# The odd side of a Fourier projection: three 128-column passes per weight tile, or one of 256 columns and one of 128

## The chip, the cores and the metric

The kernel runs on one core of a Trainium2 chip. The time is device microseconds of one execution of the program. Five engines matter here: TensorE (PE in the rows; PEld are its weight loads), VectorE (DVE), ScalarE (ACT), GpSimd (POOL) and SyncE (SP), which issues the DMAs. Each works through its own list of instructions in order and waits on semaphores where it needs another's result.

## The reference

Two layers of an encoder on 256 tokens of width 2048, in float32: a token mixer, a cross-attention on a memory, and a gated MLP. The change lies in the token mixer, in the linear map behind the Fourier branch:

```python
def fourier_mix(u):
    ug = u.astype(jnp.float32).reshape(b, s, N_FOURIER_GROUPS, FOURIER_GROUP_DIM)   # 4 groups of 256 channels
    y = jnp.fft.fft2(ug, axes=(1, 3), norm='ortho').real
    return y.reshape(b, s, F_WIDTH).astype(u.dtype)
...
    a = blocked_gqa(q, k, v) @ w_attn_o
    f = fourier_mix(uf) @ w_four_o
    g = jax.nn.sigmoid(h @ w_gate + b_gate)
    merged = g[..., :D_MODEL] * a + g[..., D_MODEL:] * f
    return merged @ w_mix_o
```

`w_four_o` has 1024 rows and 2048 columns.

## The kernel before

**Products in two halves.** Every float32 operand is split into a high part, rounded to fp32r, and a low part, the rest: `hi` and `lo`. A product is hi x hi + hi x lo + lo x hi. Weights come from HBM as tiles of 128 x 1024 (`load`, L105, four buffers `w32`), are split by ScalarE (`whi`, L121, a cast) and VectorE (`wlo`, L123, a subtraction), four buffers each, and then used as the stationary operand, 128 x 128 at a time. The activations are the moving operand and lie as [128, 2 parts, 256 tokens], so that one pass of 512 columns with the `hi` weights makes two of the three products at once, in two halves of a PSUM bank, and one pass of 256 columns with the `lo` weights makes the third (`block`, L140 and L141). `merge` (L212, L213) adds the two halves: ScalarE copies one to SBUF, VectorE adds the other.

**The Fourier branch.** The output of the two-dimensional transform has a symmetry over the tokens, so the branch keeps an even part on 129 tokens (`FE`, four groups, and `FX`, a fifth operand for the middle channels; padded to 130) and an odd part on 127 tokens (`FO`, padded to 128). Each is stored as [128, 2 parts, n]. `fourier(c)` computes 128 of the 2048 output columns. It forms sums and differences of the weights (`sd`, L754 and L755), splits them, and makes an even side with the sums (and with `FX` and a small extra weight, `wx`) and an odd side with the differences. Then f[t] = even - odd and f[256 - t] = even + odd (L782, L783), and the gate multiplies it (L786). It is a generator: at each `yield` the caller may put other work in.

In the even side a weight tile takes the two passes of `block`, 260 and 130 columns. In the odd side it takes three passes of 128 columns, (hi, part 0), (hi, part 1) and (lo, part 0), all into the same 128 columns of the same bank (L774): the bank has 512 float32 columns, of which the even side fills 260.

**Where it is called.** Two of the 16 output blocks (`EARLY`, c = 0 and 1) are computed with their gates inside attention, one `next(early)` per head, to fill TensorE there. `att_scores` makes the scores `sc` (L488) and the softmax, `att_out` transposes the probabilities (`pt`, L510), splits them (`et`, `et_lo`), multiplies by the values (`pv`, L521) and splits the result into `O`. The other 14 come after attention, in the merge loop, one turn for each c: two gate products `g` (L140, L141, 16 weight tiles each), the Fourier block, the attention projection `a` (16 weight tiles), and the merge of all into `M`.

**What sets the order.** The code is written against a framework that orders the instructions of each engine itself, by priority and by when it expects operands to be ready, and that puts in the semaphores. Tiles of a pool go round its buffers: PSUM pool `ps_mm` has four banks for `g`, `f` and `a` alike, pool `t1` five scratch buffers of 128 x 256 for gates, halves, `even`, `fo` and `ao`.

Of the kernel before, what the change touches and what calls it, by code (L numbers as in the profile page):

```python
# [16 lines left out]
P = 128  # L17
# [22 lines left out]
NE, NO = 130, 128  # L40
# [3 lines left out]
def encoder(ctx: ExitStack, tc: tile.TileContext, t, out):  # L44
    nc = tc.nc
# [42 lines left out]
    def tmp1(name, dt=F32):  # L88
        return t1.tile([P, T], dt, tag="t1", name=name)
# [4 lines left out]
    def psum(name):  # L94
        return ps_mm.tile([P, 512], F32, tag="mm", name=name)
# [4 lines left out]
    def psum_pt(name):  # L100
        return ps_pt.tile([P, 512], F32, tag="pt", name=name)

    def load(src, n=HW):
        w = wp.tile([P, HW], F32, tag="w32", name="w32", bufs=4)
        nc.sync.dma_start(w[:, :n], src)  # L105
        return w
# [465 lines left out]
    for l in range(L):  # L572
# [85 lines left out]
        for j, n, g, dst, w0 in pairs:  # L658
# [8 lines left out]
            if n is qs and j in (2, 4):  # L667

                i = j - 2
                ps = psum_pt("ps_kn")  # L670
# [13 lines left out]
        FE = [F[:, i:j].rearrange("p (s n) -> p s n", s=2) for i, j in zip(o, o[1:])]  # L684
        FX = FE.pop()
        o = [o[-1] + g * 2 * NO for g in range(5)]
        FO = [F[:, i:j].rearrange("p (s n) -> p s n", s=2) for i, j in zip(o, o[1:])]
# [61 lines left out]
        def fourier(c):  # L749


            src = load(t["w_fo"][l, c][:, :HW])
            sd = wp.tile([P, HW], F32, tag="w32", name="sd", bufs=4)
            nc.vector.tensor_add(sd[:, :512], src[:, :512], src[:, 512:])  # L754
            nc.vector.tensor_sub(sd[:, 512:], src[:, :512], src[:, 512:])  # L755
            w = Unit(None, cuts=[(0, HW)], loaded=[sd])
            w.split()
            wx = wp.tile([P, P], F32, tag="wx", name="wx")
            nc.sync.dma_start(wx, t["w_fo"][l, c][:, HW:])
            xh, xl = wx_hl[c % 2], wx_hl[2 + c % 2]  # L760
            nc.scalar.copy(xh, wx)
            nc.vector.tensor_sub(xl, wx, xh.bitcast(F32))
            ps = psum("f")
            for k in range(5):
                hi, lo = w(k * P) if k < 4 else (xh, xl)
                a = FE[k] if k < 4 else FX
                nc.tensor.matmul(ps[:, : 2 * NE], hi, a.rearrange("p s n -> p (s n)"), start=k == 0, stop=False, skip_group_check=True)
                nc.tensor.matmul(ps[:, :NE], lo, a[:, 0], start=False, stop=k == 4, skip_group_check=True)
            yield
            odd = ps[:, 2 * NE : 2 * NE + NO]  # L770
            for k in range(4):
                hi, lo = w(512 + k * P)
                for i, (x, part) in enumerate(((hi, 0), (hi, 1), (lo, 0))):
                    nc.tensor.matmul(  # L774
                        odd, x, FO[k][:, part], start=k + i == 0, stop=k == 3 and i == 2, skip_group_check=True
                    )
            yield
            even = tmp1("even")
            nc.scalar.copy(even[:, :129], ps[:, NE : NE + 129])
            nc.vector.tensor_add(even[:, :129], even[:, :129], ps[:, :129])  # L780
            f = tmp1("fo")
            nc.vector.tensor_sub(f[:, 1:128], even[:, 1:128], odd[:, :127])  # L782
            nc.vector.tensor_add(f[:, 255:128:-1], even[:, 1:128], odd[:, :127])  # L783
            nc.vector.tensor_copy(f[:, 0:129:128], even[:, 0:129:128])
            g = gates[c][1]
            nc.vector.scalar_tensor_tensor(out=g, in0=g, scalar=1.0, in1=f, op0=ALU.add, op1=ALU.mult)  # L786

        gates = [[] for _ in range(KT)]
        early = chain(*[chain(gated(c, 0), gated(c, 1), fourier(c)) for c in range(EARLY)])
        before = None  # L790
        for h in range(NH + 1):
            if h < NH:
                k = [k_hl[:, h // GRP, part] for part in range(2)]
# [20 lines left out]
        for c in range(KT):  # L814
            if c >= EARLY:
                run(chain(gated(c, 0), gated(c, 1), fourier(c)))
            scaled_split(merged(c), 0.5, M[:, c])
# [32 lines left out]
        if l == 0:  # L850
            ps = msum.ps
# [294 lines left out]
```

## Time and profile before

| what | value |
|---|---|
| runs | 3044.52, 3046.54, 3048.32 us; median 3046.54 |
| profiled execution | 3047.76 us, span 3046.0 us |
| granted TensorE clock | 0.995 of full, mean over the span |
| TensorE busy | 98% of the span |
| VectorE busy | 69% |
| ScalarE busy | 56% |

The span runs from the first to the last instruction in the trace; the time has 1.8 us more around it. Busy is the time in which an engine has at least one instruction under way; for TensorE instructions overlap, so the sum of their durations says little, and the distance from one start to the next says what a pass costs.

### The profile page before, as it was taken

Reading aid. Unit: us, or ns where it says so; the run is one execution under the profiler, and the core shown is the slowest. Engines: PE = TensorE matmul, PEld = TensorE weight load, DVE = VectorE, ACT = ScalarE, POOL = GpSimd, SP = SyncE. Lnnn points to the kernel's source line nnn. Section 1 sums busy time; section 2 is a strip of 40 time slices with the busy share of each in tenths; the row PEclk is TensorE's granted clock in tenths of the full one; section 3 lists DMA queues with packets and bytes.
Section 4 is the critical chain, followed back from the end, with each engine's and each line's share of the span. In section 5 each row is a group of like instructions: output and inputs, shape, how many; then the busy total and the mean of one; then the engine's idle time right before and its main releaser. Section 6 shows DMA issues by size and latency. Waiting matters only on the chain.

```text
span 3046.0 us, 43076 instructions
## 1 busy us (share of the span) xinstructions
PE 2981.9 (98%) x16016; PEld 2536.8 (83%) x16016; DVE 2113.3 (69%) x3358; ACT 1712.6 (56%) x2812; POOL 39.1 (1%) x40
## 2 busy tenths in 40 slices
PE   8999999999999999999989999999999999999998
PEld 6888888877788888888868888888777888888887
DVE  5678777675785766757766687776657857677676
ACT  5676544565654545545556865454657545455454
POOL 1000000010000000000000000000000000000000
PEclk9999999999999999999999999999999999999999
DMA  7543555654456565565745435556645565655655
GB/s 256 172 155 112 191 195 191 204 191 150 162 194 193 187 184 193 181 197 186 223 153 174 160 106 192 189 193 205 201 149 167 187 196 186 185 194 184 196 186 161
DMA packets 162499, 554.44 MB, mean 182 GB/s; under 512 B 18160, under 2 KB 22512, under 8 KB 162160
## 3 DMA queue, kind: packets, MB, share of 16 engines
q1 hardware_dynamic: 162288, 551.68, 56.0%
q8 instruction: 125, 2.05, 0.3%
q14 instruction: 86, 0.70, 0.1%
HBM read 549.51 MB, written 2.10 MB: 181 GB/s over the span
## 4 chain that ended last, share of the span: by engine, by line
PE 73%; DVE 2%; ACT 2%; issue 1%; DMA 0%; POOLq 0%; DVEq 0%; SPq 0%; ACTq 0%
PE up L140 21%; PE up L141 10%; PE y L342 7%; PE y L344 6%; PE y L343 6%; PE g L140 4%; PE a L140 2%; PE g L141 2%; PE qk L140 2%; DVE wlo L123 1%; PE as L344 1%; PE as L342 1%; PE a L141 1%; PE as L343 1%; PE kx L140 1%; PE as L200 1%
## 5 line engine op out<-in xcount | busy, mean ns | idle before, releaser
L123 DVE TENSOR_TENSOR wlo<-w,whi 128x1024 fp32r<-128x1024 f32 (+1 forms) x993 | 1195.6, 1208 | 699.1 <-ACT whi L121 692.4
L121 ACT CAST whi<-w 128x1024 fp32r<-128x1024 f32 (+1 forms) x993 | 1026.7, 1036 | 1008.1 <-PE up L140 385.1
L140 PE MATMUL up<-A_ff,whi 128*128 128x512 f32 x2688 | 946.6, 398 | 0.8 <-ACT whi L121 0.8
L141 PE MATMUL up<-A_ff,wlo 128*128 128x256 f32 x2688 | 752.9, 280 | 0.5 <-DVE wlo L123 0.5
L140 PEld LDWEIGHTS up<-A_ff,whi 128*128 128x128 f32 x2688 | 505.0, 188 | 125.2 <-ACT whi L121 1.6
L141 PEld LDWEIGHTS up<-A_ff,wlo 128*128 128x128 f32 x2688 | 507.1, 189 | 1.7 <-DVE wlo L123 1.4
L140 PE MATMUL g<-A_mix,whi 128*128 128x512 f32 x1024 | 365.6, 399 | 0.0
L141 PE MATMUL g<-A_mix,wlo 128*128 128x256 f32 x1024 | 288.9, 282 | 0.0
L342 PE MATMUL y<-whi,G 128*128 128x512 f32 x704 | 274.1, 389 | 0.0
L343 PE MATMUL y<-wlo,G 128*128 128x512 f32 x704 | 274.0, 389 | 0.0
L344 PE MATMUL y<-whi,G 128*128 128x512 f32 x704 | 274.0, 389 | 0.0
L140 PEld LDWEIGHTS g<-A_mix,whi 128*128 128x128 f32 x1024 | 192.5, 188 | 45.7
L140 PE MATMUL qk<-A_mix,whi 128*128 128x512 f32 x640 | 227.6, 399 | 0.0
L141 PEld LDWEIGHTS g<-A_mix,wlo 128*128 128x128 f32 x1024 | 193.6, 189 | 0.0
L140 PE MATMUL a<-O,whi 128*128 128x512 f32 x512 | 183.7, 402 | 0.0
L141 PE MATMUL qk<-A_mix,wlo 128*128 128x256 f32 x640 | 179.8, 281 | 0.0
L344 PEld LDWEIGHTS y<-whi,G 128*128 128x128 f32 x704 | 132.2, 188 | 27.6
L342 PEld LDWEIGHTS y<-whi,G 128*128 128x128 f32 x704 | 132.2, 188 | 27.5
L343 PEld LDWEIGHTS y<-wlo,G 128*128 128x128 f32 x704 | 132.1, 188 | 27.2
L141 PE MATMUL a<-O,wlo 128*128 128x256 f32 x512 | 143.8, 281 | 0.0
L140 PEld LDWEIGHTS qk<-A_mix,whi 128*128 128x128 f32 x640 | 120.2, 188 | 27.5
L141 PEld LDWEIGHTS qk<-A_mix,wlo 128*128 128x128 f32 x640 | 121.0, 189 | 0.1
(267 smaller groups left out, 4096.3 us busy)
## 6 DMA issues: line engine op xcount, KB each, us to landing
w<-in_w_up SPq DMA_DIRECT2D x336, 512.0 KB, 3.8
w<-in_w_dn SPq DMA_DIRECT2D x160, 512.0 KB, 3.8
w<-in_w_g SPq DMA_DIRECT2D x128, 512.0 KB, 4.4
w<-in_w_qk SPq DMA_DIRECT2D x80, 512.0 KB, 4.4
w<-in_w_ao SPq DMA_DIRECT2D x64, 512.0 KB, 3.7
w<-in_w_mo SPq DMA_DIRECT2D x64, 512.0 KB, 4.3
w<-in_w_vu SPq DMA_DIRECT2D x47, 512.0 KB, 4.8
w<-in_w_fo SPq DMA_DIRECT2D x32, 512.0 KB, 3.7
```

What stands on the lines that cost most here:

```text
L121: nc.scalar.copy(hi[:, :m], w[:, :m])
L123: nc.vector.tensor_sub(lo[:, :m], w[:, :m], hi[:, :m].bitcast(F32))
L140: nc.tensor.matmul(ps, hi, a, start=first, stop=False, skip_group_check=True)
L141: nc.tensor.matmul(ps[:, :T], lo, a[:, 0:T], start=False, stop=last, skip_group_check=True)
L200: nc.tensor.matmul(pss[j], ah, lo, start=False, stop=False)
L342: nc.tensor.matmul(ps, ah, hi, start=first, stop=False)
L343: nc.tensor.matmul(ps, ah, lo, start=False, stop=False)
L344: nc.tensor.matmul(ps, al, hi, start=False, stop=last)
```

## The change

The odd side gets a bank of its own (`fodd`) and the form of the even side: per weight tile one pass of 256 columns with the `hi` weights over both parts of `FO`, into two halves of that bank, and one pass of 128 columns with the `lo` weights. Both sides run in one loop, with a `yield` after each as before. Since the odd product now lies in two halves, it is brought together as the even one was: a copy by ScalarE and an add by VectorE, into a fifth kind of scratch tile, `odd`.

```diff
-            ps = psum("f")
-            for k in range(5):
-                hi, lo = w(k * P) if k < 4 else (xh, xl)
-                a = FE[k] if k < 4 else FX
-                nc.tensor.matmul(ps[:, : 2 * NE], hi, a.rearrange("p s n -> p (s n)"), start=k == 0, stop=False, skip_group_check=True)
-                nc.tensor.matmul(ps[:, :NE], lo, a[:, 0], start=False, stop=k == 4, skip_group_check=True)
-            yield
-            odd = ps[:, 2 * NE : 2 * NE + NO]
-            for k in range(4):
-                hi, lo = w(512 + k * P)
-                for i, (x, part) in enumerate(((hi, 0), (hi, 1), (lo, 0))):
+            pse, pso = psum("f"), psum("fodd")
+            for ps, ops, c0, nt in ((pse, FE + [FX], 0, NE), (pso, FO, 512, NO)):
+                for k, a in enumerate(ops):
+                    hi, lo = w(c0 + k * P) if k < 4 else (xh, xl)
                     nc.tensor.matmul(
-                        odd, x, FO[k][:, part], start=k + i == 0, stop=k == 3 and i == 2, skip_group_check=True
+                        ps[:, : 2 * nt], hi, a.rearrange("p s n -> p (s n)"), start=k == 0, stop=False, skip_group_check=True
                     )
-            yield
-            even = tmp1("even")
-            nc.scalar.copy(even[:, :129], ps[:, NE : NE + 129])
-            nc.vector.tensor_add(even[:, :129], even[:, :129], ps[:, :129])
+                    nc.tensor.matmul(
+                        ps[:, :nt], lo, a[:, 0], start=False, stop=k == len(ops) - 1, skip_group_check=True
+                    )
+                yield
+            even, odd = tmp1("even"), tmp1("odd")
+            for x, ps, nt in ((even[:, :129], pse, NE), (odd[:, :127], pso, NO)):
+                n = x.shape[1]
+                nc.scalar.copy(x, ps[:, nt : nt + n])
+                nc.vector.tensor_add(x, x, ps[:, :n])
```

The framework orders the engines anew. Three places follow, rows with - as before, with + as changed.

TensorE, in the merge loop, from the end of the even side to the first passes of `a`; the lines left out repeat the three rows of a weight tile, and then the two, for the other three tiles:

```order
-L768 MATMUL f<-F 128x130
-L774 MATMUL f<-F,whi 128x128 x2
-L774 MATMUL f<-F,wlo 128x128
...
+L770 MATMUL f<-F 128x130
+L767 MATMUL fodd<-F,whi 128x256
+L770 MATMUL fodd<-F,wlo 128x128
...
 L140 MATMUL a<-O,whi 128x512
 L141 MATMUL a<-O,wlo 128x256
```

Twelve passes per call become eight, in the same place; nothing else moves on TensorE in the merge loop.

ScalarE, in the merge loop, around the same place of the first turn (c = 2): `half<-g` is the merge of the second gate product, `F<-wx` the cast of a small weight, `w_3149` the second half of the next turn's first gate weights:

```order
 L212 COPY half<-g 128x256
 L761 CAST F<-wx 128x128
-L746 ACTIVATE gate<-gate,hb 128x256
+L777 COPY even<-f 128x129
 L121 CAST whi<-w_3149 128x1024
-L779 COPY even<-f 128x129
+L746 ACTIVATE gate<-gate,hb 128x256
+L777 COPY odd<-fodd 128x127
 L121 CAST whi<-w_3198 128x1024
 L121 CAST whi<-w_3200 128x1024
```

The copy of the even side moves ahead of that weight cast, the gate's activation behind it, and the new copy of the odd side follows.

TensorE, inside attention, the odd side of c = 0, between the scores `sc` of one head and the `pv` of another:

```order
-L774 MATMUL f<-F,whi 128x128 x2
-L774 MATMUL f<-F,wlo 128x128
-L521 MATMUL pv<-et_lo,kv 128x256 x2
-L510 MATMUL pt<-con,e 128x128 x4
-L774 MATMUL f<-F,whi 128x128 x2
-L774 MATMUL f<-F,wlo 128x128
-L774 MATMUL f<-F,whi 128x128
-L521 MATMUL pv<-et,kv 128x256 x4
-L774 MATMUL f<-F,whi 128x128
-L774 MATMUL f<-F,wlo 128x128
+L767 MATMUL fodd<-F,whi 128x256
+L770 MATMUL fodd<-F,wlo 128x128
```

The odd passes stood between the steps of attention; they now stand in one block (of which the first tile's two rows are shown), and the `pv` and `pt` steps that stood among them come later, among gate passes.

## Rows read from the trace of the kernel before

**Rows 1.** The page: busy time by engine; the chain that ended last, by engine.

```profile
PE 2981.9 (98%) x16016; PEld 2536.8 (83%) x16016; DVE 2113.3 (69%) x3358; ACT 1712.6 (56%) x2812; POOL 39.1 (1%) x40
...
PE 73%; DVE 2%; ACT 2%; issue 1%; DMA 0%; POOLq 0%; DVEq 0%; SPq 0%; ACTq 0%
```

**Rows 2.** Busy time by stretch, merge loop of each layer; stretch, its length, engines, clock.

```profile
285.00:555.00 270.00, 270.00 (x1632) 238.52 (x1631) 192.02 (x320) 133.64 (x205) 0.00 (x0) 1.00 0.58 192
1835.00:2105.00 270.00, 270.00 (x1615) 237.95 (x1614) 189.90 (x313) 132.90 (x202) 0.00 (x0) 1.00 0.59 192
```

The five numbers behind the length are PE, PEld, DVE, ACT and POOL, each with its count of instructions; then come the granted clock, the DMA share and GB/s.

**Rows 3.** The same view, around the two Fourier blocks inside attention, first layer.

```profile
240.00:255.00 15.00, 14.40 (x107) 13.16 (x106) 13.68 (x39) 10.86 (x31) 0.00 (x0) 1.00 0.23 75
275.00:285.00 10.00, 8.91 (x65) 8.09 (x65) 6.65 (x15) 5.02 (x11) 0.00 (x0) 1.00 0.34 114
```

**Rows 4.** Order of time, TensorE, c = 2: start us, duration us, engine, line, operation.

```profile
304.54 0.40 PE L140 MATMUL g<-A_mix,whi 128*128 128x512 f32 x1
304.78 0.28 PE L141 MATMUL g<-A_mix,wlo 128*128 128x256 f32 x1
304.90 0.28 PE L767 MATMUL f<-F,whi 128*128 128x260 f32 x1
305.02 0.22 PE L768 MATMUL f<-F,wlo 128*128 128x130 f32 x1
...
305.25 0.22 PE L768 MATMUL f<-F,wlo 128*128 128x130 f32 x1
305.25 0.19 PEld L767 LDWEIGHTS f<-F,whi 128*128 128x128 f32 x1
...
305.36 0.19 PEld L768 LDWEIGHTS f<-F,wlo 128*128 128x128 f32 x1
...
305.48 0.19 PEld L767 LDWEIGHTS f<-F,whi 128*128 128x128 f32 x1
...
306.00 0.38 PE L774 MATMUL f<-F,whi 128*128 128x128 f32 x2
...
306.22 0.28 PE L774 MATMUL f<-F,wlo 128*128 128x128 f32 x1
...
307.34 0.45 PE L140 MATMUL a<-O,whi 128*128 128x512 f32 x1
307.63 0.28 PE L141 MATMUL a<-O,wlo 128*128 128x256 f32 x1
```

Durations overlap; "x2" are two passes in one row, and the first of its two starts at the time shown.

**Rows 5.** Order of time, TensorE around c = 1, with idle time and releaser.

```profile
278.42 0.71 PE L521 MATMUL pv<-et,kv 128*128 128x256 f32 x4 [0.69 <-DVE O L525]
...
280.82 0.74 PE L521 MATMUL pv<-et,kv 128*128 128x256 f32 x4 [0.40 <-ACT et L513]
```

**Rows 6.** Instructions on tile `even`: count, duration ns least/median/most, first and last start.

```profile
L779 ACT COPY even<-f x32: 250/257/293, 254.3 to 2087.4; 128x129 f32<-128x129 f32 x32
L780 DVE TENSOR_TENSOR even<-even,f x32: 279/283/288, 255.9 to 2088.6; 128x129 f32<-128x129 f32 x32
```

**Rows 7.** Order of time, ScalarE, VectorE and TensorE, from c = 2 to the next gate product.

```profile
307.25 0.42 DVE L213 TENSOR_TENSOR gate<-g,half 128x256 f32<-128x256 f32 x1
308.30 0.51 ACT L746 ACTIVATE gate<-gate,hb 128x256 f32<-128x256 f32 x1 [1.76 <-DVE gate L745]
308.71 1.03 ACT L121 CAST whi<-w 128x1024 fp32r<-128x1024 f32 x1
309.77 1.23 DVE L123 TENSOR_TENSOR wlo<-w,whi 128x1024 fp32r<-128x1024 f32 x1 [1.57 <-ACT whi L121]
312.87 0.16 DVE L784 COPY fo<-even 128x2 f32<-128x2 f32 x1
313.05 0.40 PE L140 MATMUL g<-A_mix,whi 128*128 128x512 f32 x1
314.13 0.36 ACT L212 COPY half<-a 128x256 f32<-128x256 f32 x1
```

## The prediction

> **What bounds the kernel now.** I read the page first, for who is busy and which engine carries the chain that ended last: TensorE is busy 98% of the span and carries 73% of that chain [rows 1]. Since busy shares are averages, I then read the stretches where the changed code runs. `fourier(c)` is called 16 times in each of two layers. 14 of the 16 lie in the merge loop, each between two gate products and one attention projection: there TensorE is busy in 270.00 of 270.00 us in both layers, VectorE in 192, ScalarE in 134, at a granted clock of 1.00 (2.4 GHz) [rows 2]. So in that loop a nanosecond taken from TensorE's issue is a nanosecond off the end, and work on VectorE or ScalarE costs nothing as long as no matmul comes to wait for it. The other two calls (c = 0 and 1) lie inside attention, where TensorE does wait: 0.60 us of 15 and 1.09 us of 10 are idle around them, and VectorE is busy 13.68 of the 15 [rows 3].
>
> Busy time can't price the edit, because durations of matmuls overlap: a 128-column pass is 0.28 us long and starts 0.11 us after the one before it [rows 4]. What counts is start to start, so the view I price from is the order of time on TensorE and its weight loads in one call (c = 2) [rows 4].
>
> **What the rows say a pass costs.** The gate product's passes: 512 columns from 304.54 to 304.78, 0.24 us, and 256 columns from 304.78 to 304.90, 0.12 us: 0.46 ns per column, so they go by columns. The even side does not: a pair of 260 and 130 columns takes 0.23 us (130-column pass at 305.02, the next at 305.25), where 390 columns at 0.46 ns would be 0.18. Its weight loads start at 305.25, 305.36, 305.48: one every 0.115 us, without a gap. The odd side: the first of 12 passes starts at 306.00, the attention projection that follows at 307.34, so 12 passes of 128 columns take 1.34 us, 0.1117 us each, where columns alone would be 0.059. So with few columns behind each weight tile, a pass costs one weight load, about 0.112 to 0.115 us, whatever its columns; only from about 256 columns on do the columns cost as much.
>
> **The change part by part.**
>
> *TensorE, merge loop.* Per weight tile of the odd side, three passes of 128 columns (two of them with the same `hi` weights, loaded twice) become one of 256 and one of 128. Four tiles per call: 12 weight loads and passes become 8; the columns stay 384 per tile. After the change the odd side has the shape of the even side (256+128 beside 260+130), so I price a pair at that row, 0.23 us: 4 x 0.23 = 0.92 us against 1.34, **0.42 us saved per call**. Bounds: two bare loads at 0.1117 make a pair 0.223, so 0.45 us saved; at the other end a 256-column pass at its 0.12 and a 128-column pass at 0.115 make 0.235, so 0.40 [rows 4]. 28 calls x 0.42 = **11.8 us** (11.2 to 12.6). The step into the next product (first 512-column pass of `a`, 0.29 us instead of 0.235 to its partner) is there before and after alike; I take 0 for it, and at most 28 x 0.055 = 1.5 us more.
>
> The Trainium skill, "TensorE: Matmul & The Clock Gate", section "Back-to-back issue gap", gives the gap of back-to-back matmuls at full clock as columns over 2.4 GHz plus 2.5 ns, that is by columns alone. By it 384 columns before and after would differ by one 2.5 ns per tile, an estimate of 0.3 us in all: a rule against this change. The same page, section "LDWEIGHTS (loading the stationary operand)", gives a load as 128 columns at 1.2 GHz, an estimated 107 ns, with which the 0.112 to 0.115 us of the rows agrees.
>
> *TensorE, inside attention.* Four calls (two per layer). 4 x 0.42 = 1.7 us of issue goes here too, but around c = 1 the odd passes fill time in which `pv` waits for the last heads' softmax chain [rows 5], and what doesn't fill it any more becomes wait. The order also moves: in c = 0 the odd passes run as one block and no longer between the `pv` and `pt` steps, gate passes take their place later, and passes of `a` are drawn ahead of the last `pv`. Bounds from the present idle time of 0.60 + 1.09 = 1.7 us per layer [rows 3]: if it doubles, the four calls lose 3.4 - 1.7 = 1.7 us on balance; if it goes away, they gain 1.7 + 3.4 = 5.1 us. I take half of the issue time, **0.8 us**.
>
> *ScalarE and VectorE.* Per call one more copy out of PSUM (0.257 us for 129 columns) and one more add (0.283 us) [rows 6]: 32 x 0.26 = 8 us and 32 x 0.28 = 9 us over the kernel. In the merge loop these lie beside TensorE. What covers them is the lead of the weight splits: the split whose ScalarE half runs at 308.71 and whose VectorE half starts at 309.77 and lasts 1.23, so ends at 311.0 [rows 7], is the second half of the next gate product (`w_3149` in the order shown). That product starts after the 16 pairs of `a`, at 313.05, and needs its second half 8 pairs of 0.36 later, at 315.9: 4.9 us of lead. A half microsecond costs none of it that matters; the even copy even moves into the 1.76 us that ScalarE spends waiting for the gate's multiply [rows 7], and the odd one goes behind the split. With the cover gone, the price would be their whole 0.54 us, 28 x 0.54 = 15 us. Nothing is queued behind the two copies but these splits; both wait for passes that TensorE issues ahead of anything that needs the split. I take 0.
>
> *PSUM and scratch.* Five tiles per call now go round four banks (gate, gate, even, odd, `a`). The tightest turn: the first gate product takes over the bank of the second gate product of the call before, with even, odd and `a` between them, 1.1 + 0.92 + 5.7 = 7.7 us. That bank is free when the merge's add ends, 307.67 [rows 7], which is 2.6 us after the last pass of the product ended: 5 us of room. In the five scratch buffers two gates, `even`, `odd` and `fo` now live at once, so the copy of `a` must find `even` released; now that is at 313.0 and the copy at 314.1 [rows 7]. I take 0 for both.
>
> *DMA.* Nothing is added; one small load moves behind two weight loads. 0.
>
> **Sum.** 11.8 + 0.8 = 12.6 us. The profiled execution took 3047.8 us (span 3046.0, 1.8 around it), so it would take 3035.2; it stands 1.2 us over the median of the runs, 3046.54, so the median goes to **3034 us** (3046.5 - 12.6 = 3033.9).
>
> **The rivals.**
>
> 1. *By columns.* If a pass is paid by its columns, the edit saves nothing: 384 columns before and after, **3046.5 us**. For it: 512 and 256 columns do go at 0.46 ns each. Against: the 12 odd passes take 1.34 us where columns would give 0.71, and the even pairs lie at two loads. It could come in part, if the 256-column pass and its load did not overlap: a pair of 0.12 + 0.115 + 0.06 = 0.295 would leave 1.34 - 1.18 = 0.16 us per call, 4.5 us in all, **3042 us**. The trace has no sign of that in the 260-column pairs.
>
> 2. *Attention gives it back.* The block of odd passes no longer covers the waits for `et` and `O`, and each step of VectorE's almost full queue comes later. At twice what I bound it by, 3.4 us per layer more wait, the end is 3046.5 - 11.8 - 1.7 + 6.8 = **3040 us**. For it: the order there changes most, and VectorE is at 91%. Against: the idle time is only 1.7 us per layer now, and the gate passes that cover it are still there.
>
> 3. *Slower: the bank.* TensorE comes to wait at the first gate product for the bank of the second gate product of the call before. It decides from the point where that product's merge ends more than 5 us later than now: then every further microsecond costs 28 us, and 0.45 us of wait per call eats the whole gain. At 1 us of wait: 3046.5 - 12.6 + 28 = **3062 us**. For it: four banks for five tiles, and ScalarE's order puts the even copy ahead of a split and the gate behind it. Against: the room is twice the merge's present lag, and no wait on a merge shows today.
>
> **How the numbers follow.** The forecast, 0.80; columns, whole or in part, 0.06; attention gives back, 0.08; slower, 0.06. The bounds of the forecast's terms are 11.2 - 1.7 = 9.5 and 12.6 + 1.5 + 5.1 = 19.2 us, but the far end needs every wait in attention gone; with half of them gone it is 17 us: 3029.5 to 3037. Reaching a little into the second rival and allowing 2 us for the spread of the runs, the range is 3029 to 3039. A change of 0.2%, 6.1 us, is about what a measurement of this kernel can tell from none. Faster by more: 0.80 and half of rival 2 and a little of 1, 0.85. Within: 0.09. Slower: 0.06.
>
> **What would show it.** In the profile after, the odd side of a merge-loop call takes 0.90 to 0.94 us from its first pass to the first pass of `a`, its weight loads start 0.11 to 0.12 us apart, TensorE is busy without a wait in the merge loop, and the merge loop of each layer is 5.6 to 6.3 us shorter. Wrong: an odd pair at 0.29 us or more (rival 1); more than 1.7 us of idle TensorE per layer around the first two calls (rival 2); a wait of a gate or odd pass on a merge's add, or on a split (rival 3).

## The result, and the profile after

The changed kernel takes **3028.76 us** (median of 4 runs, 3028.68 to 3030.25) against 3045.53 for the kernel before beside it (4 runs, 3042.94 to 3048.32): a ratio of 0.9946, 95% interval 0.9929 to 0.9963. So it is faster, by 16.8 us where 12.6 were forecast; 3028.76 lies 0.2 us under the low end of the forecast's range. The profiled execution took 3028.68 us, its span is 3026.9.

The page has the same picture as [rows 1], with 128 passes fewer on TensorE and 32 instructions more on each of VectorE and ScalarE:

```profile
PE 2969.3 (98%) x15888; PEld 2523.7 (83%) x15888; DVE 2117.6 (70%) x3390; ACT 1720.7 (57%) x2844; POOL 40.3 (1%) x40
...
PE 73%; DVE 3%; ACT 2%; issue 1%; DMA 0%; POOLq 0%; DVEq 0%; ACTq 0%; SPq 0%
```

Busy time by stretch, the two around attention's Fourier blocks first ([rows 3]), then the merge loop of each layer ([rows 2]); its columns are those of [rows 2]:

```profile
240.00:255.00 15.00, 14.93 (x110) 13.73 (x109) 14.73 (x41) 11.39 (x34) 0.00 (x0) 1.00 0.22 71
275.00:285.00 10.00, 9.31 (x64) 8.37 (x63) 7.64 (x17) 5.80 (x13) 0.00 (x0) 1.00 0.38 136
280.00:550.00 270.00, 270.00 (x1617) 238.16 (x1617) 198.36 (x337) 140.26 (x223) 0.00 (x0) 1.00 0.58 195
1815.00:2065.00 250.00, 250.00 (x1502) 220.47 (x1501) 183.35 (x312) 130.83 (x210) 0.00 (x0) 1.00 0.58 197
```

TensorE is still busy in all of the merge loop, so VectorE's and ScalarE's new work made no matmul wait there. In attention its idle time fell, from 0.60 to 0.07 us and from 1.09 to 0.69: no wait took the place of the issue time.

The order of time on TensorE and its weight loads in one call, which answers to [rows 4]; the last line is the first even pass of the last turn:

```profile
302.50 0.28 PE L767 MATMUL f<-F,whi 128*128 128x260 f32 x1
...
303.55 0.22 PE L770 MATMUL f<-F 128*128 128x130 f32 x1
...
303.61 0.33 PE L767 MATMUL fodd<-F,whi 128*128 128x256 f32 x1
303.77 0.22 PE L770 MATMUL fodd<-F,wlo 128*128 128x128 f32 x1
303.83 0.33 PE L767 MATMUL fodd<-F,whi 128*128 128x256 f32 x1
303.88 0.19 PEld L770 LDWEIGHTS fodd<-F,wlo 128*128 128x128 f32 x1
304.00 0.19 PEld L767 LDWEIGHTS fodd<-F,whi 128*128 128x128 f32 x1
304.11 0.19 PEld L770 LDWEIGHTS fodd<-F,wlo 128*128 128x128 f32 x1
...
304.45 0.22 PE L770 MATMUL fodd<-F,wlo 128*128 128x128 f32 x1
304.51 0.45 PE L140 MATMUL a<-O,whi 128*128 128x512 f32 x1
304.80 0.28 PE L141 MATMUL a<-O,wlo 128*128 128x256 f32 x1
304.91 0.39 PE L140 MATMUL a<-O,whi 128*128 128x512 f32 x1
...
549.76 0.28 PE L767 MATMUL f<-F,whi 128*128 128x260 f32 x1
```

The odd side takes 304.51 - 303.61 = 0.90 us instead of 1.34, and its weight loads start 0.11 to 0.12 us apart. Thirteen turns, c = 2 to 15, last 549.76 - 302.50 = 247.26 us; before, that pass of the last turn stood at 557.83:

```profile
557.83 0.29 PE L767 MATMUL f<-F,whi 128*128 128x260 f32 x1
```

557.83 - 304.90 [rows 4] = 252.93 us. So a turn takes 19.020 us instead of 19.456: 0.436 less.

TensorE's waits from 225 to 300 us, all of attention's Fourier part (us in total, times, longest), of before and then of after:

```profile
PE pv L521 <- DVE O L525: 0.7, 1, 0.7
PE pv L521 <- ACT et L513: 0.7, 2, 0.4
PE pv L521 <- DVE et_lo L515: 0.3, 1, 0.3
```

```profile
PE pv L521 <- DVE O L525: 0.7, 1, 0.7
```

1.7 us of waits per layer became 0.7. The second layer's waits are the same to the tenth. Where they went shows in the order of time. Before:

```profile
250.05 0.51 PE L521 MATMUL pv<-et_lo,kv 128*128 128x256 f32 x2 [0.32 <-DVE et_lo L515]
...
251.67 0.73 PE L521 MATMUL pv<-et,kv 128*128 128x256 f32 x4 [0.28 <-ACT et L513]
```

After:

```profile
249.87 0.22 PE L770 MATMUL fodd<-F,wlo 128*128 128x128 f32 x1
250.17 0.51 PE L521 MATMUL pv<-et_lo,kv 128*128 128x256 f32 x2
...
252.96 0.28 PE L141 MATMUL g<-A_mix,wlo 128*128 128x256 f32 x1
253.07 0.67 PE L521 MATMUL pv<-et,kv 128*128 128x256 f32 x4
...
279.62 0.40 PE L140 MATMUL a<-O,whi 128*128 128x512 f32 x1
279.87 0.74 PE L521 MATMUL pv<-et,kv 128*128 128x256 f32 x4
```

The `pv` of `et_lo` starts 4.51 us after the first even pass of c = 0 in both kernels (245.54 and 245.66 us). Before, two of the four odd tiles were done by then and TensorE waited 0.32 us; now all four are done. The `pv` that waited 0.28 us now stands behind eight gate passes, and the last one, which waited 0.40 us [rows 5], behind three passes of `a`. So the new order put other work into these three waits. Only that second `pv` came to stand among gate passes: the first, with its `pt`, follows right behind the odd block.

**Where the 19.1 us between the two profiled executions lie**, by first even passes of calls in TensorE's order of time: merge loop 28 calls x 0.436 = 12.2; attention, from c = 0 to c = 2, 59.36 to 56.84 us in the first layer and 59.41 to 56.89 in the second, so 2 x 2.52 = 5.0; and 1.9 in stretches where nothing is edited (1.7 of it between the layers), by which single executions differ anyway. 12.2 + 5.0 = 17.2, beside 16.8 by the medians.

The new work on the tile `odd` (tile view: count, duration ns least, median and most, first and last start), for [rows 6]:

```profile
L777 ACT COPY odd<-fodd x32: 243/246/277, 250.1 to 2068.1; 128x127 f32<-128x127 f32 x32
L778 DVE TENSOR_TENSOR odd<-odd,fodd x32: 275/278/280, 251.5 to 2068.8; 128x127 f32<-128x127 f32 x32
```

### The profile page after: what moved, and what is told of

Its sections match the earlier page's. It is cut to its first block, busy times and chain, and to the rows that moved or that the text cites. A ratio compares the mean times of both kernels' runs of the same rounds, so it can differ in the third digit from the quotient of the medians.

```text
span 3026.9 us, 42856 instructions
## 1 busy us (share of the span) xinstructions
PE 2969.3 (98%) x15888; PEld 2523.7 (83%) x15888; DVE 2117.6 (70%) x3390; ACT 1720.7 (57%) x2844; POOL 40.3 (1%) x40
## 4 chain that ended last, share of the span: by engine, by line
PE 73%; DVE 3%; ACT 2%; issue 1%; DMA 0%; POOLq 0%; DVEq 0%; ACTq 0%; SPq 0%
PE up L140 21%; PE up L141 10%; PE y L342 6%; PE y L343 6%; PE y L344 6%; PE g L140 4%; PE a L140 2%; PE g L141 2%; PE qk L140 2%; DVE wlo L123 1%; PE as L344 1%; PE as L342 1%; PE a L141 1%; PE as L343 1%; PE kx L140 1%; PE as L200 1%
```

## The experiments

The theory at the start: with few columns behind a weight tile a pass costs one weight load, so the merge loop's gain is the four loads saved per call; attention's gain is issue time plus waits that the new order removed. The rival: the gain comes from the bank of its own, or from the order, and the number of passes matters little.

In the table "c0 to c2" is the time from the first even pass of c = 0 to that of c = 2 in the first layer (the second layer's differs by at most 0.11, but for lo_first_all, where it is 0.39 longer), "waits" what the view of TensorE's waits lists from 225 to 300 us (single waits above 0.15 us), "pair" the time from one 512-column pass to the next in the stretch behind c = 1, "turn" the mean of the turns c = 2 to 15 of the first layer. Ratios are to the kernel before, run beside each.

| kernel | us | ratio (95%) | c0 to c2 | waits | pair | turn |
|---|---|---|---|---|---|---|
| before | 3045.5 | 1 | 59.36 | 1.7 | 0.353 | 19.456 |
| after | 3028.8 | 0.9946 (0.9929 to 0.9963) | 56.84 | 0.7 | 0.347 | 19.020 |
| merge_only | 3034.3 | 0.9955 (0.9942 to 0.9967) | 58.95 | 1.7 | 0.347 | 19.020 |
| attn_only | 3044.1 | 0.9988 (0.9979 to 0.9997) | 57.27 | 0.7 | 0.353 | 19.456 |
| three_passes_own_bank | 3046.4 | 0.9995 (0.9986 to 1.0004) | 58.67 | 1.4 | 0.347 | 19.456 |
| wide_lo | 3029.3 | 0.9943 (0.9928 to 0.9958) | 55.91 | 0.0 | 0.347 | 19.060 |
| even_three | 3049.2 | 1.0001 (0.9991 to 1.0010) | 60.17 | 2.5 | 0.353 | 19.408 |
| no_odd_merge | 3028.9 | 0.9934 (0.9919 to 0.9949) | 56.67 | 0.5 | 0.353 | 19.020 |
| one_yield | 3027.3 | 0.9930 (0.9915 to 0.9944) | 57.24 | 0.5 | 0.353 | 18.998 |
| extra_yield | 3031.3 | 0.9940 (0.9925 to 0.9954) | 57.23 | 0.9 | 0.353 | 19.020 |
| lo_first_a | 3021.9 | 0.9914 (0.9900 to 0.9929) | 57.24 | 0.7 | 0.353 | 18.721 |
| lo_first_all | 3023.1 | 0.9918 (0.9901 to 0.9934) | 57.21 | 0.6 | 0.347 | 18.720 |
| lo_first_a_up | 3008.3 | 0.9873 (0.9856 to 0.9889) | 56.91 | 0.7 | 0.347 | 18.719 |

**The change in the merge loop alone, and in attention alone.**

```diff
+            if c >= EARLY:      # attn_only: c < EARLY
                 pse, pso = psum("f"), psum("fodd")
...
+            else:
+                ps = psum("f")
...
```

The other branch holds the lines of before.

> The new odd side only in the merge loop (28 calls); the 4 calls in attention keep the old three passes and the old shared bank, and the order in attention is word for word that of the kernel before. Theory (weight loads set the pace of small passes, and attention adds its own gain through its order and waits): a turn of the merge loop from first even pass to first even pass 19.02 us, as after (19.455 before); from the first even pass of c = 0 to that of c = 2 59.4 us, as before; time 3045.5 - 28 x 0.435 = 3033.3. Rival (attention owes its gain to nothing of its own, the whole is a faster run of the merge loop and what follows): 3029 to 3030.

> The reverse: the new odd side only in the 4 calls inside attention, with the order there word for word that of the changed kernel; the merge loop as before. Theory: turn 19.455 us, c = 0 to c = 2 56.85 us per layer, time 3045.5 - 2 x 2.52 = 3040.5. If the attention part is only the issue that is saved, 4 x 0.44 = 1.8 us: 3043.7, and c = 0 to c = 2 58.5 us.

The two parts add up: 13.5 us and 3.7 us by the medians, 17.2 together. merge_only has the turn of after, and TensorE's order and waits of before in attention; its 59.36 - 58.95 = 0.41 us there is pace alone (below). attn_only has the turn of before.

**Three passes, but in the new bank and loop.**

```diff
-                    nc.tensor.matmul(
-                        ps[:, : 2 * nt], hi, a.rearrange("p s n -> p (s n)"), start=k == 0, stop=False, skip_group_check=True
-                    )
+                    passes = ((hi, 0, 0, nt), (hi, 1, nt, 2 * nt), (lo, 0, 0, nt)) if ps is pso else ((hi, slice(0, 2), 0, 2 * nt), (lo, 0, 0, nt))
...
```

> The changed kernel, but the 256-column pass of the odd side is split again into two of 128 with the same weights, into the two halves of the odd bank: 12 loads per call again, with the bank, the copy, the add and the columns of the changed kernel. Loads set the pace: odd side 1.34 us, turn 19.46 us, time 3043 to 3045.5 depending on attention. Columns set the pace: odd side 0.90, turn 19.02, time 3029.

The order of time on TensorE, the odd side of c = 2 of this kernel ("x2" are the two `hi` passes of a tile):

```profile
306.05 0.39 PE L771 MATMUL fodd<-F,whi 128*128 128x128 f32 x2
306.27 0.28 PE L771 MATMUL fodd<-F,wlo 128*128 128x128 f32 x1
...
307.39 0.45 PE L140 MATMUL a<-O,whi 128*128 128x512 f32 x1
```

307.39 - 306.05 = 1.34 us, and the turn is 19.456, as before. The bank, the copy and the add are those of after; only the passes are back. So the merge loop's gain is the passes, and the bank neither gives nor costs anything.

**More columns in the same number of passes**: the `lo` pass of the odd side over all 256 columns, which computes one product more than the kernel needs.

```diff
+                    wide = 2 * nt if ps is pso else nt
...
-                        ps[:, :nt], lo, a[:, 0], start=False, stop=k == len(ops) - 1, skip_group_check=True
+                    nc.tensor.matmul(ps[:, :wide], lo, flat_a[:, :wide], start=False, stop=k == len(ops) - 1, skip_group_check=True)
```

> The changed kernel, but the pass with the lo weights runs over all 256 columns too (it adds lo x lo): 8 loads per call as in the changed kernel, 128 columns more per tile. Loads set the pace: the wider pass fits under the load, a pair goes from 0.225 to at most 0.238 us (two 256-column passes at 0.119), turn 19.02 to 19.07, time 3029 to 3030.5. Columns set the pace: 4 x 128 x 0.46 ns = 0.235 us per call, turn 19.26, time 3036.

Its odd side in the order of time:

```profile
302.59 0.33 PE L769 MATMUL fodd<-F,whi 128*128 128x256 f32 x1
302.76 0.28 PE L770 MATMUL fodd<-F,wlo 128*128 128x256 f32 x1
...
303.59 0.40 PE L140 MATMUL a<-O,whi 128*128 128x512 f32 x1
303.82 0.28 PE L141 MATMUL a<-O,wlo 128*128 128x256 f32 x1
```

512 more columns per call make the odd side 303.59 - 302.59 = 1.00 us instead of 0.90, where 0.46 ns per column would add 0.24. More than half of that comes back at once: `a`'s first pass leads its partner by 303.82 - 303.59 = 0.23 us instead of 304.80 - 304.51 = 0.29. The turn is 0.04 longer.

**Three passes on the even side** instead (the edit of the run above with `ps is pse`).

> The changed kernel, but the even side takes three passes of 130 columns per tile instead of 260 and 130: 5 loads more per call, the same columns. Loads set the pace: an even triple at 3 x 0.1117 to 3 x 0.115 = 0.335 to 0.345 us instead of 0.23, so 0.53 to 0.57 us more per call, turn 19.55 to 19.6, time 3028.8 + 28 x 0.55 + attention (4 x 0.55) = about 3046. Columns set the pace: 19.02 and 3029.

The other side of the same coin: five weight loads more per call, and the whole gain is gone. Where the stretch behind it has pairs at 0.353, a turn takes 19.545 us, 0.53 more than in after. It has 2.5 us of waits per layer in attention too. By the table's ratios it stands 0.55% over after, 16.8 us; its turns and its two attention stretches are 28 x 0.38 + 2 x 3.3 = 17.2 us longer.

**Without the odd side's copy and add.**

```diff
-            even, odd = tmp1("even"), tmp1("odd")
-            for x, ps, nt in ((even[:, :129], pse, NE), (odd[:, :127], pso, NO)):
+            even, odd = tmp1("even"), pso
+            for x, ps, nt in ((even[:, :129], pse, NE),):
```

> The changed kernel without the copy and the add that bring the two halves of the odd bank together; the subtraction and addition read the first half in PSUM. It leaves out the product hi x lo of the odd side. Theory (both lie under TensorE's work): turn 19.02 us, attention within 0.5 us of the changed kernel, time 3028 to 3029.5. Rival (the two cost something in attention, where VectorE is over 90% busy): turn 19.02, c = 0 to c = 2 shorter by up to 2 x 0.54 us per layer, time about 3026.6. If they cost in the merge loop too: turn shorter than 18.9.

The turn stays 19.020: in the merge loop the copies and adds (32 of each in the kernel, 16.8 us of engine time) lie wholly beside TensorE. In attention that isn't shown: c0 to c2 is 0.60 us shorter than in attn_only, which has the same pair, but TensorE's order there is another.

**Other places to yield**: one `yield` behind both sides (one_yield), or one more in the middle of each side in attention (extra_yield).

```diff
+                    if c < EARLY and k == 1:      # extra_yield
+                        yield
-                yield
+            yield      # one_yield
```

> The changed kernel without the yield between the even and the odd side: the same instructions, another order inside attention only. If the attention part of the gain is saved issue alone, c = 0 to c = 2 stays at 56.85 us per layer within 0.2 and the time at 3028.8; if order and cover decide, it moves by 0.3 us or more per layer, to either side, with the turn at 19.02.

> The changed kernel with one yield more, in the middle of the odd side of c = 0 and 1: the odd passes are spread among the attention steps again, as they were before, with 8 passes and not 12. If saved issue alone makes the attention part, c = 0 to c = 2 stays at 56.85 us per layer within 0.2; if the block order makes it, part of the waits comes back, 57.3 to 58.5 us per layer and 3030 to 3032. Turn 19.02 either way.

These were to show whether the block of odd passes, that is the order, took the waits away. They can't, for neither brings the old order back. In extra_yield the odd passes of c = 0 still stand in one block, from 248.10 us on, all ahead of the `pv` of `et_lo`:

```profile
248.97 0.22 PE L770 MATMUL fodd<-F,wlo 128*128 128x128 f32 x1
249.38 0.51 PE L521 MATMUL pv<-et_lo,kv 128*128 128x256 f32 x2 [0.19 <-DVE et_lo L515]
```

The last `pv` stands behind three passes of `a` there too. Waits are 0.5 and 0.9 us per layer, beside 0.7 of after; that c0 to c2 is 0.4 us longer than in after is the pace of the pairs, taken up next. Of the runs with the new bank in attention, those with two passes on both sides have 0 to 0.9 us of waits per layer, and those with three on one side 1.4 to 2.5; but the number of passes and the order changed together. Three passes and two were never run in one order of attention, so what each is worth there isn't settled.

**What sets the pace of the long products.** The table's column "pair" has two values, and nothing between. They were not in any theory so far; merge_only's 0.41 us in attention is 62 pairs at 0.353 against 0.347, with nothing changed ahead of them on TensorE. In even_three they alternate from turn to turn, and one_yield's 18.998 is one turn of 18.72, its first, and twelve of 19.02. One kernel tried several openings at once, one turn each, seven in the first layer and eight in the second (S1, S2: one or two odd tiles in three passes; E1: one even tile in three; B: the last odd tile `lo` first; G: the last gate tile `lo` first; A: the first tile of `a` `lo` first):

```diff
+    {3: "S1", 5: "S1", 6: "S1", 8: "S2", 10: "A", 12: "A", 13: "A"},
+    {3: "B", 5: "B", 6: "B", 8: "E1", 10: "E1", 11: "E1", 13: "G", 14: "G"},
```

> The changed kernel with one small edit in some turns of the merge loop, to find what sets the pace of the long product passes (pairs of 512 and 256 columns went at 0.3533 us per pair in most stretches and at 0.3467 in some, as in every second turn of even_three, which has 23 short passes per turn where the changed kernel has 18). First layer: c = 3, 5, 6 one 256-column odd pass split in two of 128 (19 short passes), c = 8 two split (20), c = 10, 12, 13 the first tile of the attention projection with its lo pass ahead of its hi pass. Second layer: c = 3, 5, 6 the last odd tile lo ahead of hi, c = 8, 10, 11 one 260-column even pass split in two (19), c = 13, 14 the last tile of the second gate product lo ahead of hi. Theory count: an odd number of short passes switches the pace behind it, so c = 3, 5 of the first and c = 8, 10 of the second layer are followed by 46 pairs at 0.3467, the reorderings and c = 8 of the first layer by 0.3533. Rival seam: the order at the seam decides, the reordered turns change and the split ones do not. Rival chance: no turn follows its edit, the pace comes from waits. A turn at 0.3467 is 46 x 0.0066 = 0.30 us shorter than its own edit makes it.

It took 3031.62 us in its one run (3046.47 for before). That the parity of the passes decides fell: 19 short passes (S1 and E1) ran on at 0.353, 20 (S2) at 0.347, but the even count of after runs at 0.353. B stayed at 0.353 all three times; G gave 0.347 once and 0.353 once. `a`'s first tile with its 256-column `lo` pass ahead of the 512-column one gave 0.347 three times out of three. So that was done in every turn (lo_first_a). In another kernel (lo_first_all) the two lines of `block` itself are swapped, so that every tile of every such product has `lo` first. The edit of lo_first_a:

```diff
+    def block_lo_first(ps, w, col, a, first, last):
+
+        if not first:
+            return block(ps, w, col, a, first, last)
+        hi, lo = w(col)
+        nc.tensor.matmul(ps[:, :T], lo, a[:, 0:T], start=True, stop=False, skip_group_check=True)
+        nc.tensor.matmul(ps, hi, a, start=False, stop=last, skip_group_check=True)
...
+            merge(ws_chunk(t["w_ao"][l, c], O, KT, name="a", blk=block_lo_first), a)
```

> The changed kernel, with the first weight tile of every attention projection taking its 256-column lo pass ahead of its 512-column hi pass; nothing else. If the pace of the long stretch behind the short passes is set by which pass opens it, as in c = 10, 12, 13 of pace_probe: 46 pairs per turn at 0.3467 and not 0.3533, turn 18.72 us for 19.02, time 3028.8 - 27 x 0.30 = about 3020.7. If those three turns were chance: turn 19.02, 3028.8.

> The changed kernel, with the lo pass ahead of the hi pass in every tile of every such product (gates, q and k, attention projection, memory keys, up-projection). If the opening pass sets the pace everywhere: turn 18.72 us, and the three long stretches of the up-projection in each layer that go at 0.3533 now (351, 351 and 319 pairs) at 0.3467 too, 2 x 1021 x 0.0066 = 13.5 us, time about 3007 to 3012. If it does so only behind short passes, the up-projection, which follows passes of 512 columns, stays at 0.3533: about 3021. If the seam into the Fourier block matters (its first pass then follows a 512-column pass), turn 19.02 again or between.

The seam in lo_first_a, in the order of time (of the later pairs only the 512-column passes are shown):

```profile
304.74 0.22 PE L778 MATMUL fodd<-F,wlo 128*128 128x128 f32 x1
304.80 0.33 PE L148 MATMUL a<-O,wlo 128*128 128x256 f32 x1
304.97 0.39 PE L149 MATMUL a<-O,whi 128*128 128x512 f32 x1
305.20 0.40 PE L140 MATMUL a<-O,whi 128*128 128x512 f32 x1
...
305.56 0.39 PE L140 MATMUL a<-O,whi 128*128 128x512 f32 x1
...
305.91 0.39 PE L140 MATMUL a<-O,whi 128*128 128x512 f32 x1
```

and after's at the same place, once it runs steadily:

```profile
308.09 0.40 PE L140 MATMUL a<-O,whi 128*128 128x512 f32 x1
...
308.44 0.40 PE L140 MATMUL a<-O,whi 128*128 128x512 f32 x1
...
308.80 0.40 PE L140 MATMUL a<-O,whi 128*128 128x512 f32 x1
...
309.15 0.40 PE L140 MATMUL a<-O,whi 128*128 128x512 f32 x1
```

All turns from c = 2 on take 18.72 us, 0.30 less than in after. `lo` first everywhere gives no more: the up-projection, whose openings stand behind 512-column passes, stays at 0.353. It was given short passes of its own, at the three openings whose long stretches had run at 0.353:

```diff
...
+        if col == 0:
+            nc.tensor.matmul(ps, hi, a, start=True, stop=False, skip_group_check=True)
+            for o in (0, P):
+                nc.tensor.matmul(ps[:, o : o + P], lo, a[:, o : o + P], start=False, stop=False, skip_group_check=True)
+        elif col == P:
+            nc.tensor.matmul(ps[:, :T], lo, a[:, 0:T], start=False, stop=False, skip_group_check=True)
+            nc.tensor.matmul(ps, hi, a, start=False, stop=last, skip_group_check=True)
...
```

> lo_first_a, and the same opening made by hand ahead of the three long stretches of the up-projection in each layer that go at 0.3533 per pair behind the 512-column passes of the down-projection: in the first weight tile the lo pass is cut into two of 128 columns, the second tile takes lo ahead of hi. The cut costs one load more, 6 x 0.11 = 0.7 us. If two short passes and a 256-column opening set the pace wherever they stand: 351, 351 and 319 pairs at 0.3467, 2 x 1021 x 0.0066 - 0.7 = 12.8 us, time 3021.9 - 12.8 = about 3009. If the opening works only behind the long chain of short passes of the Fourier block, where the weight loads have caught up with the passes: the stretches stay at 0.3533 and the time at 3022 to 3023.

The opening at 966 us in the order of time, and the line of all up-projection passes in the tile view (durations as above); then the same line of after:

```profile
966.12 0.33 PE L157 MATMUL up<-A_ff,wlo 128*128 128x128 f32 x2
966.29 0.33 PE L159 MATMUL up<-A_ff,wlo 128*128 128x256 f32 x1
966.46 0.40 PE L160 MATMUL up<-A_ff,whi 128*128 128x512 f32 x1
```

```profile
L140 PE MATMUL up<-A_ff,whi x2676: 390/391/503, 790.0 to 2936.3; 128*128 128x512 f32 x192
```

```profile
L140 PE MATMUL up<-A_ff,whi x2688: 389/398/507, 794.1 to 2956.6; 128*128 128x512 f32 x192
```

The stretches of 349, 349 and 317 pairs behind these openings go at 0.347 in both layers, and the median 512-column pass is 391 ns instead of 398. **3008.32 us** (3008.18 to 3009.56), 1.3% under the kernel before and 0.73% under after (by the ratios): the version that beats both.

## Why the prediction was right, and where it was off

The change is faster, through the term that the forecast was built on. The time lies just under the range because the term for attention was sized too small.

- **TensorE, merge loop.** Right in mechanism and nearly in size: 0.436 us per call, 12.2 in all, where 0.42 and 11.8 stood (bounds 11.2 to 12.6). The pair is 0.225, nearer to two bare loads than to the even side's 0.23. Three_passes_own_bank and wide_lo show that passes are paid, each with its weight load, and hardly their columns. That it is the load, the rows of after support: a pass can start 0.06 us behind another (303.77 to 303.83), so 0.112 us is no least distance of two passes, while the loads keep their 0.11 to 0.12 us. No run has a pass without a load of its own (15888 of each in after), so the two were not tried apart.
- **Rival 1, by columns.** Fell: an odd pass costs 0.112 us at 128 columns each (1.34 / 12) and at 256 and 128 in turn (0.90 / 8), and at 256 each it costs 0.125 (wide_lo, 1.00 / 8). The Trainium skill, "TensorE: Matmul & The Clock Gate", section "Back-to-back issue gap", was read too narrowly for this rival: its formula by columns stands there for an isolated gap, and the section itself says that the formula falls short for few columns, since in a stream the weight load counts too. The trace agrees with that. The section's figure for such a stream, 81 ns at 128 columns, is not met here: the runs show 112.
- **Attention: the mis-sized term.** The step "I take half of the issue time, 0.8 us" failed: 5.0 us came, at the upper bound of 5.1. These 4.2 us, and 0.4 from the term above, are what 17.2 has over the 12.6 forecast. I let saved issue turn into wait and gave the new order no term of its own. In its place, per layer: 0.88 us of issue saved in full, 1.0 us of waits gone (1.7 to 0.7), because the new order has odd, gate and `a` passes where TensorE waited, 0.41 by the pace behind c = 1, and 0.2 that the view of waits doesn't show. That the sum meets the bound is luck: the bound had all 3.4 us of waits gone, and 2.0 went; 0.8 in both layers is pace, which no run ties to the edit (merge_only has it without the new form there, attn_only has the new form without it). Issue, waits and pace together give 57.07 for the measured 56.84, 57.48 for attn_only's 57.27, and exactly merge_only's 58.95; in wide_lo, no_odd_merge and extra_yield 0.4 to 0.7 us stays unexplained. **Rival 2** had the opposite sign of what happened.
- **ScalarE, VectorE.** Right in the merge loop: nothing, by no_odd_merge's equal turn. In attention their price was not shown. That the lead of the weight splits is the cover was not tried.
- **PSUM and scratch, rival 3.** Right: TensorE has no wait in the merge loop, and three_passes_own_bank, with the same banks, has the turn of before.
- **The step into `a`.** It was taken as 0 (at most 1.5 us), rightly: it is 0.29 us in after too, and there is nothing in it to win. From the last odd pass to the second 512-column pass of `a` are 0.46 us in after (304.45 to 304.91), and 0.46 in lo_first_a (304.74 to 305.20), which opens `a` otherwise and has no such step; what the `lo`-first kernels gain comes behind it.
- **What would show it.** All four marks came as written. The loop got shorter by 13 x 0.436 + 0.44 = 6.1 us per layer, within 5.6 to 6.3, and the odd side takes 0.90 us, the low end of its 0.90 to 0.94; the loads start 0.11 to 0.12 us apart, and TensorE has no wait there. One sum was a little short: the far end of 19.2 us without half of the 3.4 us of waits is 17.5, not 17, which gives 3029.0 where 3029.5 stood.

## What to carry to other kernels

On an engine that never waits, price a matmul pass from start to start at its own column count: below about 256 columns behind each new weight tile it costs a weight load, so join passes that share weights until the columns cost as much as the load. In a stretch where the engine does wait, don't assume that saved issue becomes wait: read the waits by releaser, look what the new order puts ahead of each, and keep both signs in the sum. And compare the steady interval of equal passes in different stretches of one trace; here two intervals 2% apart were worth more than the change.

## What the runs showed of the hardware that was not expected

Long rows of 512- and 256-column pairs run at one of two steady intervals, 0.3533 or 0.3467 us per pair, held over up to 351 pairs, at a granted clock of 1.00 and without waits. In the kernel before the whole merge loop is at 0.3533, and of the up-projection's long stretches one of 302 pairs is at 0.3467 and three of 351, 351 and 319 are at 0.3533, in both layers. Short passes followed by a 256-column pass, then the 512-column ones, gave 0.3467 wherever they opened a product in the merge loop or one of the three long stretches of the up-projection: 0.30 us less per turn (7.8 us in the 26 turns from c = 2 to 15), and 2 x 1015 x 0.0066 = 13.4 us in the up-projection. Behind c = 1, where `pv` passes stand between the first pairs of `a`, that opening came out at either (lo_first_a 0.353, lo_first_a_up 0.347). In pace_probe and lo_first_all that stretch has one interval in the first layer and the other in the second. Why there are two intervals, and why that stretch differs between kernels and layers with the same TensorE order up to it (before and merge_only for one pair), stays open.
